# GpSimd subtracts weights instead of scaling probabilities in a two-layer attention and MLP trunk, with projection blocks in another order

## The chip, the cores and the metric

The kernel runs on one core of one Trainium2 chip. The metric is the device time of one execution in microseconds (us). The kernel before takes 627.66 us, the median of three runs (627.09 to 627.96).

## What is computed

The reference is a trunk of two layers on 256 tokens of width 1024, all in float32. A layer normalizes its input, projects it to 2848 columns, runs two kinds of attention on the parts, projects the result back, and follows with an MLP whose activation is a squared ReLU:

```python
for l in range(DEPTH):                                   # DEPTH = 2
    h = _rms_norm(x, g_pre_mix[l])
    parts = jnp.split(h @ w_in[l], split_at, axis=-1)
    nq, kc, vc, ksel, vsel, kwin, vwin, gates, fq, fk, fv, ff = parts
    ...
    mix = jnp.concatenate([o_nsa, o_fox], axis=-1) @ w_out[l]
    x = x + _rms_norm(mix, g_post_mix[l])
    h = _rms_norm(x, g_pre_mlp[l])
    y = jnp.square(jax.nn.relu(h @ w_up[l])) @ w_down[l]
    x = x + _rms_norm(y, g_post_mlp[l])
```

The first kind of attention, "nsa", has eight heads of 64 columns in two groups. Each head adds three branches, each with a gate: attention to compressed keys and values (16 blocks, made by a small network with a GELU), to selected keys and to a window; with 256 tokens the last two see all earlier tokens, with different keys and values. The second kind, "fox", has eight heads with a decay that comes from running sums of forget gates. Queries and keys of nsa are rotated by position (RoPE).

## The kernel before, in words

**Products of float32 by three passes.** TensorE multiplies numbers in a shorter format (fp32r). A weight tile `wraw`, loaded by DMA, is therefore split: ScalarE copies it to `whi` in the short format, VectorE subtracts `wraw - whi` into `wlo` (`Weights.get`, L625; the subtraction is L648). Activations are split alike (`split`, L807). A product is the sum of three: high by high, high by low, low by high.

**The projection in blocks.** The first 2048 of the projection's columns come in 16 blocks of 128 (`block`, L1254): each is 8 matmuls of 512 columns with `whi` (which do both halves of the activation at once) and 8 of 256 with `wlo`, into one of two `acc` buffers of PSUM. The block is evacuated by a ScalarE copy and a VectorE add (`both_halves`, L970) to its home (`block_home`, L1192); only then is its `acc` buffer free for the block after next. The homes in order are `kT` (blocks 0, 1: selected and window keys), `cT` (2, 3: what the compressed keys and values are made of), `qT` (4 to 7: queries, two heads each), then `fqT` and `fkT` (8 to 15). In layer 0 the first four blocks are computed together while data arrives (`first_chunks`); in layer 1 the first two (`by_token`).

**Rotation** (`turned`, L976) of a pair of blocks takes a VectorE product `m`, a shuffle of it, a GpSimd product `y`, a VectorE sum, and a split into `kx` (keys) or `qS` (queries). `rCS` holds the cosines and sines times the norm of each token, and is made once in a layer.

**Attention** runs over 24 entries (`flat`): 16 of nsa, for four pairs of heads, two heads and two branches, then eight of fox. For each, `scores` (L1365) makes the scores of a pair on TensorE (the `kx,qS` or `cum` and `fkT,fqT` matmuls), subtracts the maximum on VectorE and exponentiates on ScalarE; `scale` (L1387) takes reciprocals and scales the probabilities `pr` in two pieces, 128x128 and 128x256; `probs_T` (L1403) transposes them on TensorE (`s<-cst,pr`); `values` multiplies by the values (`o<-prT`, `o<-prX`). The scaling is on GpSimd for fox and for the window branch (L1392, L1400), on ScalarE for the other. Between the steps `fill(n)` gives TensorE parts of the stream of blocks, of a last projection chunk (`c5`) and of the output projection; `fill_to(b)` gives it all up to block b. The compression steps (`side`, L1501) come at entries given by `SIDE`. The weights `cmp_w1` of the compression's network ride behind the blocks listed in `SEQ`.

**The order of all this is planned.** The code only records operations. `Recorder.order` then simulates the five engines with a price for every operation (`_cost`, L578), tries 140 orders with random shifts, and emits the best; each engine runs its instructions strictly in that order. So a change of a price or of the recorded sequence moves instructions on every engine. Prices in it know nothing of one engine that holds another off.

All instructions are recorded by one helper, so that almost every row of the profile has the line L535; tiles tell them apart.

Of the kernel before, what the change touches and what calls it, by code (L numbers as in the profile page):

```python
# [38 lines left out]
SEQ = range(7, 15), range(4, 12)  # L39
SIDE = (2, 7), (1, 5)  # L40
PV1 = 12
# [17 lines left out]
TM = FM + 288, FM + 512  # L59
TURNED = [i ^ 8 if i < 16 else i for i in range(32)]  # L60
# [517 lines left out]
def _cost(op, views):  # L578
    out = op.args[0] if op.args else op.kw["out"]
    n = int(np.prod(out.shape[1:]))  # L580
    if op.engine == "sync":
        v = views[0][1]
        return v.shape[0] * int(np.prod(v.shape[1:])) * 4 / 320.0
    if op.engine == "tensor":
        if op.name == "stretch":
            if op.args[2][0][0] == "transpose":
                return 108.0 * len(op.args[2])

            tiles = [_shape(x[1][1]) for x in op.args[2]]
            return sum((x[1][0].ix.size / (2.4 if x[1][1].dtype == F32R else 0.6) + 20) / (P // min(t))  # L590
                       for x, t in zip(op.args[2], tiles)) + RETILE * sum(a != b for a, b in zip(tiles, tiles[1:]))
        if op.name == "transpose":
            return 83.0 if op.args[1].dtype == F32R else 108.0
        if op.args[1].dtype == F32R:
            return 13.6 + n / 2.4
        return max(220.0, 3 + n / 0.6)
    if op.engine == "gpsimd":
        return 160 + n * (2.2 if op.name.startswith("tensor_tensor") or op.name == "tensor_mul" else 1.0)
    if op.engine == "vector":
        if op.name == "reciprocal":  # L600
            return 60 + 6.5 * n
        if op.name == "tensor_reduce":
            n = int(np.prod(op.args[1].shape[1:]))
        fast = op.name in ("tensor_copy", "tensor_scalar", "memset") and not any(v.buf.psum for _, v in views)
        aps = sum(isinstance(v, View) for v in op.args[2:4]) if op.name == "tensor_scalar" else int(
            op.name == "scalar_tensor_tensor" and isinstance(op.args[2], View))
        return 68 + 64 * aps + n * (0.52 if fast else 1.04) + 10 * (op.name == "tensor_tensor_reduce")
    src = op.args[1]
    aps = sum(isinstance(op.kw.get(k), View) for k in ("bias", "scale", "accum_out"))
    return n / 1.2 + (55 if src.buf.psum else 92) + 93 * aps  # L610


class Weights:
# [11 lines left out]
    def get(self, i):  # L625
# [14 lines left out]
        for j in range(shape[0]) if i < 2 * len(FIRSTS) else [slice(None)]:  # L640
# [7 lines left out]
            nc.vector.tensor_sub(lo[:, j], raw[:, j], hi[:, j].bitcast(F32))  # L648
# [16 lines left out]
def trunk(nc, A, consts_in, out, sbp, pp):  # L665
# [260 lines left out]
    for l in range(DEPTH):  # L926
# [47 lines left out]
        two = lambda x: x[:, None, :].to_broadcast([P, 2, S])  # L974

        def turned(src, hi, lo):  # L976

            m = tokt("m").rearrange("p (b n) -> p b n", b=2)
            y = tokt("y").rearrange("p (b n) -> p b n", b=2)
            nc.vector.tensor_mul(m, src, two(T["rS"]))  # L980
            nc.vector.stream_shuffle(m, m, TURNED)
            nc.gpsimd.tensor_mul(y, src, two(T["rC"]))
# [209 lines left out]
        def block_home(b):  # L1192

            name = ("kT", "cT", "qT", "qT", "fqT", "fqT", "fkT", "fkT")[b // 2]
            if name not in T:
                if b < 4:
                    T[name] = tokt(name).rearrange("p (b n) -> p b n", b=2)
                else:
                    T[name] = qT_tile(name)
# [4 lines left out]
            return T[name][:, b % 2 if b < 4 else b % 4, :]  # L1204

        def block_done(b):

            if b >= 8 and b % 2:
                d = T["fqT" if b < 12 else "fkT"][:, b % 4 - 1:b % 4 + 1, :]
                nc.vector.tensor_mul(d, T["u"], two(T["r"]))  # L1210
            if b in (5, 7):
                if b == 5:
                    T["qS"] = tile([P, 2, 4, S], F32R, name="qS", tag="gain")
                turned(T["qT"][:, b - 5:b - 3, :], *[T["qS"][:, j, b - 5:b - 3, :] for j in range(2)])
# [271 lines left out]
        b2k = rows[:, 36:37]  # L1486
        fill(4)
        turned(T["kT"], *kx)
        if not first:
            fill_to(3)  # L1490
        fill(4)
        gather_blocks(0)
        fill(4)
        gather_blocks(1)
        fill_to(5)
        fill(2)
# [6 lines left out]
                cv + 2: lambda: (compressed_T(), hidden_gelu("v")), cv + 3: compressed_v, 12: lambda: fill_to(NB - 1),  # L1503
                13: forget_sums, 16: lambda: fill_to("c5")}
# [5 lines left out]
        for i in range(len(flat) + 4):  # L1510
# [16 lines left out]
            fill(1)  # L1527
# [167 lines left out]
def layouts(a):  # L1695
# [6 lines left out]
    w = np.concatenate([ks, kw, kc, vc, by_head(q, 2), fox[:, :, :1024], vs, vw, by_head(g, 2), ff, fox[:, :, 1024:]],  # L1702
# [38 lines left out]
```

## Time and profile before

| what | value |
|---|---|
| median of three runs | 627.66 us |
| the profiled execution's own time | 628.2 us |
| its span, first to last instruction | 626.4 us |
| granted TensorE clock | 0.997 |
| TensorE's weight loads busy | 504.6 us, 81% |
| GpSimd busy | 78.6 us, 94 instructions |
| loaded from HBM | 114.30 MB |
| chain that ended last | PE 82%, DVE 7%, ACT 5%, issue 2%, POOL 2%, DMA 1% |

In the rows PE is TensorE's matmuls, PEld its weight loads, DVE VectorE, ACT ScalarE, POOL GpSimd. A row of a group names its output and inputs, their shapes and the count, then the busy us and the mean ns of one, then the engine's idle us just before them and what ended most of it. A row of the timeline begins with its start and its length in us; idle time ahead of it stands in brackets. Busy time of TensorE overlaps from matmul to matmul, and its ends are modelled.

### The profile page before, as it was taken

To read this page: it belongs to the slowest core of one execution; us is meant where nothing else is said; L and a number is where in the kernel's file an instruction comes from. 1 tells how busy PE (TensorE), PEld (TensorE's weight loads), DVE (VectorE), ACT (ScalarE), POOL (GpSimd) and SP (SyncE) were. 2 spreads that over 40 slices of the span, in tenths; PEclk is the share of its full clock that TensorE was granted. 3 is DMA by queue.
4 is the path that set the end of the run, shared out by engine and by line. 5 is a ranking of instruction groups with operands and counts; after the bars stand their busy time and mean duration, and the time that the engine had idled before them with its cause. 6 is when DMAs were issued, how large, how long until landed. Compare 5 with 4: busy or idle time off the path is not lost.

```text
span 626.4 us, 9901 instructions
## 1 busy us (share of the span) xinstructions
PE 608.8 (97%) x3488; PEld 504.6 (81%) x3488; DVE 457.9 (73%) x967; ACT 390.7 (62%) x802; POOL 78.6 (13%) x94
## 2 busy tenths in 40 slices
PE   9989999999999999999999999999999999999995
PEld 8867776678888888888888778867888888888884
DVE  6899985579976566566599998674997666566544
ACT  6768987467665455455466697874776555555422
POOL 0225124500000000000003432362000000000000
PEclk9999999999999999999999999999999999999998
DMA  8967774317756556555327657342486566555101
GB/s 287 402 239 257 296 225 135 102 35 265 261 190 204 188 181 201 193 182 187 133 83 253 236 171 275 102 169 68 131 290 211 176 196 202 180 191 203 37 0 68
DMA packets 36354, 115.99 MB, mean 185 GB/s; under 512 B 4432, under 2 KB 6224, under 8 KB 36304
## 3 DMA queue, kind: packets, MB, share of 16 engines
q1 hardware_dynamic: 36304, 115.36, 54.0%
q8 instruction: 27, 0.44, 0.3%
q14 instruction: 23, 0.19, 0.1%
HBM read 114.30 MB, written 1.05 MB: 184 GB/s over the span
## 4 chain that ended last, share of the span: by engine, by line
PE 82%; DVE 7%; ACT 5%; issue 2%; POOL 2%; DMA 1%; POOLq 0%; DVEq 0%; ACTq 0%
PE s L535 33%; PE acc L535 24%; PE x L535 18%; PE o L535 7%; POOL pr L535 2%; DVE wlo L535 2%; ACT whi L535 1%; ACT pr L535 1%; DVE m L535 1%; DMA wraw<-in_w_fm_dram 1%; DVE pr L535 1%; ACT rl L535 1%; ACT kstk L535 0%; DMA wraw<-in_w_dram 0%; POOLq L1737 0%
## 5 line engine op out<-in xcount | busy, mean ns | idle before, releaser
L535 DVE TENSOR_TENSOR wlo<-wraw,whi 128x1024 fp32r<-128x1024 f32 (+2 forms) x200 | 231.7, 1164 | 96.9 <-ACT whi L535 96.3
L535 ACT ACTIVATE whi<-wraw 128x1024 fp32r<-128x1024 f32 (+3 forms) x200 | 199.8, 1006 | 128.0 <-PE acc L535 61.4
L535 PE MATMUL s<-xT,whi 128*128 128x512 f32 x448 | 111.9, 392 | 0.0
L535 PEld LDWEIGHTS s<-xT,whi 128*128 128x128 f32 x448 | 81.4, 189 | 15.1
L535 PE MATMUL acc<-whi,aT 128*128 128x512 f32 x256 | 88.5, 390 | 0.0
L535 PE MATMUL x<-whi,aT 128*128 128x512 f32 x256 | 88.4, 390 | 0.0
L535 PE MATMUL acc<-xT,whi 128*128 128x512 f32 (+1 forms) x258 | 66.4, 385 | 2.7 <-DVE qT L535 2.0
L535 PEld LDWEIGHTS s<-xT,wlo 128*128 128x128 f32 x448 | 61.1, 190 | 4.4
L535 PE MATMUL s<-xT,wlo 128*128 128x256 f32 x448 | 62.5, 282 | 0.0
L535 ACT ACTIVATE pr<-pr,st 128x256 f32<-128x256 f32 (+1 forms) x128 | 55.3, 448 | 5.7 <-DVE st L535 5.4
L535 PEld LDWEIGHTS acc<-whi,aT 128*128 128x128 f32 x256 | 48.1, 188 | 10.0
L535 PEld LDWEIGHTS x<-whi,aT 128*128 128x128 f32 x256 | 48.1, 188 | 9.7
L535 PEld LDWEIGHTS acc<-xT,whi 128*128 128x128 f32 x258 | 43.6, 189 | 11.8 <-DVE qT L535 2.2
L535 PE MATMUL x<-wlo,aT 128*128 128x512 f32 x128 | 50.0, 390 | 0.0
L535 PE MATMUL acc<-wlo,aT 128*128 128x512 f32 x128 | 49.8, 389 | 0.0
L535 PE MATMUL acc<-xT,wlo 128*128 128x256 f32 x240 | 36.7, 284 | 0.0
L535 PEld LDWEIGHTS acc<-xT,wlo 128*128 128x128 f32 x240 | 33.3, 190 | 2.2 <-issue 0.4
L535 POOL TENSOR_TENSOR y<-kT,rCS 128x512 f32<-128x512 f32 x2 | 5.0, 2483 | 239.9 <-DVE rCS L535 239.9
L535 POOL TENSOR_SCALAR pr<-pr,st,gate 128x256 f32<-128x256 f32 (+1 forms) x32 | 25.7, 814 | 62.0 <-DVE st L535 56.0
L535 POOL TENSOR_SCALAR pr<-pr,st 128x128 f32<-128x128 f32 (+1 forms) x32 | 30.3, 964 | 22.3 <-DVE st L535 18.8
L535 PE MATMUL s<-cst,pr 128*128 128x128 f32 x144 | 24.3, 281 | 5.5 <-POOL pr L535 4.9
L535 ACT ACTIVATE rl<-h 128x512 f32<-128x512 f32 x28 | 17.5, 624 | 18.0 <-DVE h L535 18.0
(226 smaller groups left out, 921.9 us busy)
## 6 DMA issues: line engine op xcount, KB each, us to landing
wraw<-in_w_up_dram SPq DMA_DIRECT2D x64, 512.0 KB, 3.9
wraw<-in_w_down_dram SPq DMA_DIRECT2D x64, 512.0 KB, 3.5
wraw<-in_w_fm_dram SPq DMA_DIRECT2D x28, 512.0 KB, 6.3
wraw<-in_w_out_dram SPq DMA_DIRECT2D x16, 512.0 KB, 7.3
wraw<-in_w_dram SPq DMA_DIRECT2D x9, 512.0 KB, 4.0
w<-in_cmp_w_k_dram SPq DMA_DIRECT2D x8, 512.0 KB, 5.3
w<-in_cmp_w_v_dram SPq DMA_DIRECT2D x8, 512.0 KB, 6.4
wraw<-in_w_dram SPq DMA_DIRECT2D x6, 256.0 KB, 4.1
```

The lines of the kernel that those rows point to most:

```text
L535: getattr(getattr(self.nc, op.engine), name)(*[real(v) for v in args], **{k: real(v) for k, v in kw.items()})
```

## The change

It has six parts.

- `scale`: the scalings that GpSimd did, 64 instructions, are VectorE's. `turned`: the product `y`, six instructions, is VectorE's too.
- `Weights.get`: of blocks 7, 9, 11, 13 and 15 of each layer GpSimd does the subtraction `wraw - whi`, ten instructions of 128x1024.
- `HOMES`: the projection's columns are reordered so that block 3 is the first pair of queries and block 4 the compressed values; `fill_to((3, 5, 7, 7)[pair])` and a rotation of queries in pieces of one, one and two blocks (`q_turned`) follow from that.
- The compression's weights ride behind blocks 4 to 11 in layer 0 too, and its steps start at entries 4 and 9 in both layers.
- fox's scores call for their two blocks themselves (`fill_to(12 + (pair | 1))`), `c5` is called for at entry 18, the first nsa product by values comes at entry 14, and two parts of the stream are given at a step instead of one.
- `_cost`: GpSimd's instructions have other prices.

```diff
-SEQ = range(7, 15), range(4, 12)
-SIDE = (2, 7), (1, 5)
-PV1 = 12
+SEQ = range(4, 12), range(4, 12)
+SIDE = (4, 9), (4, 9)
+PV1 = 14
...
+HOMES = [("kT", 0), ("kT", 1), ("cT", 0), ("qT", 0), ("cT", 1), ("qT", 1), ("qT", 2), ("qT", 3)]
+HOMES += [(name, i) for name in ("fqT", "fkT") for i in range(4)]
...
-        return 160 + n * (2.2 if op.name.startswith("tensor_tensor") or op.name == "tensor_mul" else 1.0)
+        return {"tensor_mul": 700 + 2.5 * n, "tensor_sub": 700 + 3.2 * n, "tensor_copy": 600}.get(op.name, 550 + 2.2 * n)
...
-            nc.vector.tensor_sub(lo[:, j], raw[:, j], hi[:, j].bitcast(F32))
+            (nc.gpsimd if kind == "shared" else nc.vector).tensor_sub(lo[:, j], raw[:, j], hi[:, j].bitcast(F32))
...
-                add_unit((l, "in", c, q), [8, P], A["w_fm"][l, q])
+                add_unit((l, "in", c, q), [8, P], A["w_fm"][l, q], "shared" if q > 5 and q % 2 else "split")
...
-            nc.gpsimd.tensor_mul(y, src, two(T["rC"]))
+            nc.vector.tensor_mul(y, src, two(T["rC"], n))
...
-                turned(T["qT"][:, b - 5:b - 3, :], *[T["qS"][:, j, b - 5:b - 3, :] for j in range(2)])
+                q_turned(*((1, 2) if b == 5 else (2, 4)))
...
+                    fill_to(12 + (pair | 1))
...
-                    fill_to(4 + (pair | 1))
+                    fill_to((3, 5, 7, 7)[pair])
...
-                    nc.gpsimd.tensor_scalar(p[:, a:b], p[:, a:b], st[:, 2 + t:3 + t], None, op0=OP.mult)
+                    nc.vector.tensor_scalar(p[:, a:b], p[:, a:b], st[:, 2 + t:3 + t], None, op0=OP.mult)
...
-                    nc.gpsimd.tensor_scalar(p[:, a:b], p[:, a:b], st[:, 2 + t:3 + t], gate[t][:, c:c + 1],
+                    nc.vector.tensor_scalar(p[:, a:b], p[:, a:b], st[:, 2 + t:3 + t], gate[t][:, c:c + 1],
...
-        fill_to(5)
-        fill(2)
+        fill(8)
...
-                cv + 2: lambda: (compressed_T(), hidden_gelu("v")), cv + 3: compressed_v, 12: lambda: fill_to(NB - 1),
-                13: forget_sums, 16: lambda: fill_to("c5")}
+                cv + 2: lambda: (compressed_T(), hidden_gelu("v")), cv + 3: compressed_v,
+                13: forget_sums, 18: lambda: fill_to("c5")}
...
-            fill(1)
+            fill(2)
```

What this makes of the emitted order is shown at three places. First GpSimd, in layer 0 from its first instruction on tensors: rotations `y`, copies that gather `kstk` and `kstv` for the compression, and the scalings of `pr`. Before:

```order
L535 TENSOR_TENSOR y<-kT,rCS 128x512
L535 COPY kstk<-rows 128x32
L535 COPY kstv<-rows 128x32
L535 TENSOR_TENSOR y<-qT,rCS 128x512
L535 COPY kstk<-cT 64x8x15 x4
L535 COPY kstk<-rows 128x32
L535 TENSOR_SCALAR pr<-pr,st,gate 128x256
L535 TENSOR_SCALAR pr<-pr,st,gate 128x128
L535 COPY kstv<-cT 64x8x15 x4
```

After, from the same place (the first `wlo` is that of block 7, the next three of blocks 9, 11 and 13, then 15 and layer 1's 7):

```order
L537 TENSOR_TENSOR wlo<-wraw,whi 128x1024
L537 COPY kstk<-rows 128x32
L537 COPY kstv<-rows 128x32
L537 COPY kstk<-cT 64x8x15 x4
L537 COPY kstv<-cT 64x8x15 x4
L537 COPY kstk<-rows 128x32
L537 TENSOR_TENSOR wlo<-wraw,whi 128x1024 x3
L537 COPY kstv<-rows 128x32
L537 TENSOR_TENSOR wlo<-wraw,whi 128x1024 x2
```

The `y` and the scalings are gone from GpSimd, and a subtraction stands ahead of its first copy. Second, VectorE in layer 0 from `rCS` on, where keys and the first queries are rotated and blocks are evacuated (`qT<-acc`). Before:

```order
L535 TENSOR_TENSOR rCS<-cst,rT 128x512
L535 TENSOR_TENSOR wlo<-wraw,whi 128x1024
L535 TENSOR_TENSOR m<-kT,rCS 128x512
L535 TENSOR_TENSOR qT<-acc,qT 128x256
L535 TENSOR_TENSOR wlo<-wraw,whi 128x1024
L535 TENSOR_TENSOR m<-qT,rCS 128x512
L535 STREAM_SHUFFLE m<-m 128x512 x2
L535 TENSOR_TENSOR y<-y,m 128x512 x2
L535 TENSOR_TENSOR qT<-acc,qT 128x256
L535 TENSOR_TENSOR kx<-y,kx 128x512
L535 TENSOR_TENSOR qS<-y,qS 128x512
```

After, from the same `rCS` to the first evacuation behind it, that of block 5:

```order
L537 TENSOR_TENSOR rCS<-cst,rT 128x512
L537 TENSOR_TENSOR wlo<-wraw,whi 128x1024
L537 TENSOR_TENSOR m<-kT,rCS 128x512
L537 TENSOR_TENSOR y<-kT,rCS 128x512
L537 STREAM_SHUFFLE m<-m 128x512
L537 TENSOR_TENSOR m<-qT,rCS 128x256
L537 TENSOR_TENSOR y<-y,m 128x512
L537 STREAM_SHUFFLE m<-m 128x256
L537 TENSOR_TENSOR y<-qT,rCS 128x256
L537 TENSOR_TENSOR qT<-acc,qT 128x256
```

Before, that evacuation stands behind one `m`, after behind two `m`, two `y` and the shuffles; the rotation of the queries has half the width. Third, TensorE where the first pair's scores (`kx,qS`) stand in layer 0. Before, in block 8:

```order
L535 MATMUL acc<-xT,whi 128x512 x6
L535 MATMUL s<-kx,qS 128x256 x6
L535 MATMUL x<-kx,qS 128x512 x6
L535 MATMUL acc<-xT,whi 128x512 x2
L535 MATMUL acc<-xT,wlo 128x256 x8
L535 MATMUL o<-w_325,kstk 32x256 x4
```

After, in block 7 (the first row is its `whi` part):

```order
L537 MATMUL acc<-xT,whi 128x512 x8
L537 MATMUL acc<-xT,wlo 128x256 x3
L537 MATMUL s<-kx,qS 128x256 x6
L537 MATMUL x<-kx,qS 128x512 x6
L537 MATMUL acc<-xT,wlo 128x256 x5
L537 MATMUL acc<-xT,whi 128x512 x4
L537 MATMUL o<-w_345,kstk 32x256 x4
```

The scores stand five `wlo` and six `whi` matmuls earlier, and the first matmuls of the compression's network (`w,kstk`) come in the middle of block 8 instead of behind it.

More of the change, by code (lines that the diff above doesn't have):

```diff
@@ L972, in both_halves @@
             nc.vector.tensor_add(dst, ps[:, :S], dst)
-        two = lambda x: x[:, None, :].to_broadcast([P, 2, S])
+        two = lambda x, n=2: x[:, None, :].to_broadcast([P, n, S])
         def turned(src, hi, lo):
-            m = tokt("m").rearrange("p (b n) -> p b n", b=2)
-            y = tokt("y").rearrange("p (b n) -> p b n", b=2)
-            nc.vector.tensor_mul(m, src, two(T["rS"]))
+            n = src.shape[1]
+            m, y = (tokt(x)[:, :n * S].rearrange("p (b n) -> p b n", b=n) for x in "my")
+            nc.vector.tensor_mul(m, src, two(T["rS"], n))
             nc.vector.stream_shuffle(m, m, TURNED)
-            nc.gpsimd.tensor_mul(y, src, two(T["rC"]))
+            nc.vector.tensor_mul(y, src, two(T["rC"], n))
             nc.vector.tensor_add(y, y, m)
@@ L1192, in block_home @@
         def block_home(b):
-            name = ("kT", "cT", "qT", "qT", "fqT", "fqT", "fkT", "fkT")[b // 2]
+            name, i = HOMES[b]
             if name not in T:
[L1196 to L1199, printed above, removed]
+                T[name] = tokt(name).rearrange("p (b n) -> p b n", b=2) if name in ("kT", "cT") else qT_tile(name)
             if b >= 8:
@@ L1203, in block_home, with q_turned @@
                 return T["u"][:, b % 2, :]
-            return T[name][:, b % 2 if b < 4 else b % 4, :]
+            return T[name][:, i, :]
         def block_done(b):
             if b >= 8 and b % 2:
-                d = T["fqT" if b < 12 else "fkT"][:, b % 4 - 1:b % 4 + 1, :]
-                nc.vector.tensor_mul(d, T["u"], two(T["r"]))
+                name, i = HOMES[b]
+                nc.vector.tensor_mul(T[name][:, i - 1:i + 1, :], T["u"], two(T["r"]))
             if b in (5, 7):
-                if b == 5:
-                    T["qS"] = tile([P, 2, 4, S], F32R, name="qS", tag="gain")
-                turned(T["qT"][:, b - 5:b - 3, :], *[T["qS"][:, j, b - 5:b - 3, :] for j in range(2)])
+                q_turned(*((1, 2) if b == 5 else (2, 4)))
+        def q_turned(a, b):
+            if a == 0:
+                T["qS"] = tile([P, 2, 4, S], F32R, name="qS", tag="gain")
+            turned(T["qT"][:, a:b, :], *[T["qS"][:, j, a:b, :] for j in range(2)])
         def first_chunks():
@@ L1305, in part @@
                 done.add(name)
+            done.update(range(4 if first else 2))
             for b in range(4 if first else 2, NB):
@@ L1486, in trunk @@
         b2k = rows[:, 36:37]
+        if not first:
+            fill_to(2)
         fill(4)
@@ L1490, in trunk @@
             fill_to(3)
+        q_turned(0, 1)
         fill(4)
         gather_blocks(0)
-        fill(4)
+        fill_to(4)
         gather_blocks(1)
-        fill_to(5)
-        fill(2)
+        fill(8)
         flat = [("nsa", pair, par, br) for pair in range(4) for par in range(2) for br in (1, 2)]
@@ L1701, in layouts @@
     by_head = lambda x, axis: np.take(x.reshape(*x.shape[:axis], 8, -1, *x.shape[axis + 1:]), order, axis=axis).reshape(x.shape)
-    w = np.concatenate([ks, kw, kc, vc, by_head(q, 2), fox[:, :, :1024], vs, vw, by_head(g, 2), ff, fox[:, :, 1024:]],
+    q = by_head(q, 2)
+    w = np.concatenate([ks, kw, kc, q[:, :, :128], vc, q[:, :, 128:], fox[:, :, :1024], vs, vw, by_head(g, 2), ff, fox[:, :, 1024:]],
                        axis=2)
```

## The prediction

> **What bounds the kernel now.** I read the page's busy table first, then the windows by stage, then TensorE's own waits, then the timeline at the longest of them.
>
> ```profile
> PE 608.8 (97%) x3488; PEld 504.6 (81%) x3488; DVE 457.9 (73%) x967; ACT 390.7 (62%) x802; POOL 78.6 (13%) x94
> ```
>
> TensorE is busy for 608.8 of 626.4 us, so a change that leaves its matmuls alone can win at most its 17.6 idle us. The windows (columns: stage, length, then busy us of PE, PEld, DVE, ACT, POOL, the granted clock, DMA share and GB/s) say where those are. 25 to 135 us is the attention of layer 0, 335 to 435 us that of layer 1, and what follows each is MLP.
>
> ```profile
> 25.00:50.00 25.00, 21.02 (x147) 16.80 (x146) 24.19 (x59) 16.77 (x41) 10.37 (x12) 1.00 0.79 294
> 50.00:100.00 50.00, 50.00 (x350) 39.67 (x350) 45.19 (x147) 44.63 (x119) 13.99 (x20) 1.00 0.73 249
> 100.00:135.00 35.00, 32.95 (x213) 23.59 (x211) 19.52 (x58) 21.63 (x61) 13.90 (x16) 1.00 0.25 82
> 135.00:335.00 200.00, 199.90 (x1027) 170.69 (x1027) 146.50 (x217) 114.76 (x178) 0.00 (x0) 1.00 0.56 187
> 335.00:360.00 25.00, 24.14 (x165) 19.49 (x164) 23.53 (x72) 15.38 (x45) 12.41 (x13) 1.00 0.65 231
> 360.00:400.00 40.00, 40.00 (x319) 33.15 (x320) 34.13 (x123) 34.27 (x102) 10.67 (x13) 1.00 0.58 201
> 400.00:435.00 35.00, 32.73 (x217) 23.80 (x214) 19.82 (x54) 23.05 (x60) 17.08 (x18) 1.00 0.36 121
> ```
>
> TensorE idles in four of them: 4.0 us in 25 to 50, 2.1 in 100 to 135, 0.9 in 335 to 360, 2.3 in 400 to 435. In the first and third VectorE is full (24.2 and 23.5 of 25 us); in the second and fourth nobody is, so there a chain of latencies is late. The MLP has nothing to win. TensorE's waits, with total us, times and the longest:
>
> ```profile
> PE s L535 <- POOL pr L535: 4.9, 6, 1.2
> PE acc L535 <- DVE qT L535: 2.0, 1, 2.0
> PE acc L535 <- ACT whi L535: 0.8, 1, 0.8
> PE s L535 <- ACT pr L535: 0.5, 1, 0.5
> PE s L535 <- DVE hs L535: 0.4, 1, 0.4
> ```
>
> These five rows, 8.6 us, are all that this change can reach. The timeline of TensorE places the first three:
>
> ```profile
> 31.29 2.00 PE L535 MATMUL acc<-xT,whi 128*128 128x512 f32 x8
> 33.13 1.11 PE L535 MATMUL acc<-xT,wlo 128*128 128x256 f32 x8
> 36.22 1.65 PE L535 MATMUL acc<-xT,whi 128*128 128x512 f32 x6 [1.98 <-DVE qT L535]
> 49.76 0.55 PE L535 MATMUL s<-cst,pr 128*128 128x128 f32 x3 [1.25 <-POOL pr L535]
> ```
>
> 1.25 of the 4.9 us behind GpSimd's `pr` stand in the crowded start of layer 0; the other five waits, 3.65 us, are the ends of the two attentions. Why the wait for `qT` is there shows on VectorE and GpSimd in the same microseconds:
>
> ```profile
> 26.66 0.68 DVE L535 TENSOR_TENSOR rCS<-cst,rT 128x512 f32<-128x512 f32 x1
> 27.26 1.23 DVE L535 TENSOR_TENSOR wlo<-wraw,whi 128x1024 fp32r<-128x1024 f32 x1
> 28.41 1.79 DVE L535 TENSOR_TENSOR m<-kT,rCS 128x512 f32<-128x512 f32 x1
> 27.42 2.22 POOL L535 TENSOR_TENSOR y<-kT,rCS 128x512 f32<-128x512 f32 x1 [27.00 <-DVE rCS L535]
> L535 DVE TENSOR_TENSOR m<-qT,rCS x4: 626/1224/1781, 31.6 to 351.4; 128x512 f32<-128x512 f32 x4
> 52.32 1.29 POOL L535 TENSOR_TENSOR y<-qT,rCS 128x512 f32<-128x512 f32 x1
> 52.51 1.15 DVE L535 TENSOR_SCALAR gz<-gz 128x64 f32<-128x64 f32 x1
> 55.69 0.19 DVE L535 TENSOR_SCALAR gz<-gz 128x64 f32<-128x64 f32 x1
> ```
>
> VectorE's multiply `m` of 512 columns takes between 626 and 1781 ns. The long ones ran beside GpSimd's `y`: `y` was issued at 27.42, sat through VectorE's `wlo`, won the moment that ended (28.49), ran 1.15 us to 29.64, and `m` came after. A one-input `gz` of 64 columns, 0.19 us alone, took 1.15 beside a `y`. So one instruction holds the other off for its whole length, and a GpSimd two-input instruction costs VectorE up to 1781 - 626 = 1155 ns per 512 columns. The two held `m` (2.2 us) are the 1.98 us for which TensorE waited: the `qT` evacuation that frees its accumulator is queued behind them.
>
> **The change part by part.** (1) *Scaling of probabilities moves from GpSimd to VectorE*, 64 instructions, and six `y` with it.
>
> ```profile
> L535 POOL TENSOR_SCALAR pr<-pr,st 128x256 f32<-128x256 f32 x16 | 17.6, 1106 | 9.5 <-DVE st L535 6.0 <-PE acc L535 3.5
> L535 POOL TENSOR_SCALAR pr<-pr,st 128x128 f32<-128x128 f32 x16 | 13.1, 822 | 12.8 <-DVE st L535 12.8
> L535 DVE COPY hs<-o 128x256 f32<-128x256 f32 x4 | 1.7, 415 | 0.0
> L535 DVE TENSOR_SCALAR vS<-o,rsqrt 128x128 f32<-128x128 f32 x2 | 0.7, 344 | 0.0
> L535 DVE TENSOR_TENSOR wlo<-wraw,whi 128x1024 fp32r<-128x1024 f32 x180 | 220.0, 1226 | 95.2 <-ACT whi L535 94.8
> L535 DVE TENSOR_TENSOR y<-y,m 128x512 f32<-128x512 f32 x6 | 4.0, 679 | 0.0
> L535 DVE STREAM_SHUFFLE m<-m 128x512 f32<-128x512 f32 x6 | 4.3, 741 | 0.0
> ```
>
> On GpSimd a head's two scalings follow each other, 1106 + 822 = 1.93 us. VectorE has no SBUF scaling of these sizes in the trace. From below the 64-column `gz`, 0.19, bounds each of the two; from above the 256-column copy and the 128-column scaling out of PSUM, 0.42 + 0.34 = 0.76 us a head; I take 0.55, nearer the upper rows. So the chain of each scaled head is about 1.4 us shorter, while VectorE gets 32 x 0.55 = 17.6 us more work (12 to 24), and 6 x 0.68 = 4.1 for `y`. At the two ends VectorE is busy 19.5 and 19.8 of 35 us, which covers its half. The 3.65 us of waits there go; what is late next is the last pair's scaling behind `xo` and the gains product in VectorE's queue, which I price at 0.5 (0 to 3.65).
>
> (2) *Ten `wlo` subtractions move to GpSimd.* VectorE is rid of 10 x 1.23 = 12.3 us. A GpSimd subtraction of 1024 columns is not in the trace; by the `y` rows it holds VectorE for 2 x 1.15 = 2.3 us, an estimate, at worst, and for nothing where VectorE is just then at work on PSUM. Queued behind a held VectorE instruction is all of its queue, the accumulator evacuations among it, and for those TensorE waits. [...]
>
> (3) *The new order at the start of layer 0*, the place that matters most.
>
> ```profile
> 26.18 2.00 ACT L535 ACTIVATE whi<-wraw 128x1024 fp32r<-128x1024 f32 x2
> 334.27 0.68 DVE L535 TENSOR_TENSOR rCS<-cst,rT 128x512 f32<-128x512 f32 x1
> 342.91 2.00 PE L535 MATMUL acc<-xT,whi 128*128 128x512 f32 x8
> ```
>
> VectorE's chain up to the evacuation of block 5 (`qT<-acc` after the products for `kT` and the first query block) now holds their `y` too. A VectorE row starts some 0.08 us before the one ahead of it ends (26.66 + 0.68 against 27.26), so the steps are `rCS` 0.60, `wlo` 1.15, `m` and `y` 0.60 each, shuffle 0.65, a 256-column `m` 0.33 (the 415 ns of the copy less 0.08), the sum into `y` 0.60, half a shuffle 0.40, a 256-column `y` 0.33: 5.26 us. From 26.66 that is 31.9, and with the evacuation's 0.41 it is 32.3. TensorE reaches block 7 at 31.29 and needs that accumulator for it. So it waits 1.1 us even if nobody holds VectorE. GpSimd's first subtraction is block 7's; its `whi` is the second of ScalarE's two from 26.18 and done at 28.2, while VectorE is in `wlo`, just the spot in which `y` won before. I charge the full 2.3: 3.4 us of wait at block 7 (1.1 to 3.4) where 1.98 stood at block 8. The scores are then ready with block 7's third `wlo` matmul, as the order has them: nothing more.
>
> (4) *The first pair's probabilities in layer 0.* The 1.25 us behind `pr` go. VectorE's scaling is ready about 0.5 us before TensorE wants it, if the second subtraction (block 9) doesn't fall into those microseconds; if it does, 1.8 us are lost. I take 0.7. Of the 0.8 us behind `whi` I keep 0.2, since TensorE reaches block 9 later.
>
> (5) *Layer 1's start.* From `rCS` at 334.27 seventeen instructions, 7.1 us by the same steps, stand ahead of the evacuation that block 6 needs: it ends at 341.7, and TensorE comes at 342.91. With 1.2 us to spare the 0.9 us of waits there go; a full hold leaves 1.1. I take 0.8 for all.
>
> (6) *The middle stretches* (50 to 100, 360 to 400) had no wait, with VectorE idle for 4.8 and 5.9 us. Seven subtractions fall in these or near their edges. What they take from VectorE beyond what they relieve, 2.3 - 1.23 = 1.1 us each, is covered by that idle time; without that cover it is 7.7 us. I take 0.6.
>
> (7) *The rest*: compression steps at other turns, loads in another sequence (the eight `cmp_w` blocks ride earlier) and GpSimd's new planning prices touch only order. DMA is 79% busy in 25 to 50 us and nothing of TensorE waits for a landing there, so I cost them at nothing; if that cover fails, a late block costs about the 0.8 us that one `whi` cost.
>
> Sum: waits after = 3.4 + 0.7 + 0.2 + 0.8 + 0.6 + 0.5 = 6.2 us for 8.6, a gain of 2.4. The profiled execution took 628.2 us (1.8 outside its span), so 625.8 by its own time; it lies 0.54 over the median of 627.66, which gives **625.3 us**.
>
> **The rivals.** *Holds decide (slower).* Nine subtractions besides block 7's cost TensorE what they net cost VectorE: 9 x 1.1 = 9.9 us in place of the 2.1 that I gave them. Waits become 14.0, the time 628.2 + 5.4 - 0.54 = 633.1; at half that price 628.1. It is slower by the bound below from 0.64 us per subtraction on. For it: VectorE is full in the two starts (24.2 and 23.5 of 25 us) and is given 22 us more while relieved of 12. Against: TensorE had not one wait in 50 to 100 us with VectorE at 90%. Chance 0.21.
>
> *The waits change names (no change).* At the ends TensorE waits as long for VectorE's `pr`, because in-order VectorE puts `xo`, gains and `wlo` ahead of it, or layer 0's start costs 2 us more than I gave it. Waits stay near 8.6: 627.7. For it: the ends are chains, where the next link is always close. Against: 1.4 us less per head in them. Chance 0.21.
>
> *GpSimd does the waiting (faster still).* If VectorE wins the lock whenever both want it, the holds vanish from its side, and only 1.1 + 0.2 + 0.5 remain: 8.6 - 1.8 = 6.8 us gained, 620.9.
>
> ```profile
> 404.10 5.59 POOL L535 TENSOR_SCALAR pr<-pr,st 128x256 f32<-128x256 f32 x4 [3.40 <-DVE st L535]
> 405.58 3.72 DVE L535 TENSOR_TENSOR wlo<-wraw,whi 128x1024 fp32r<-128x1024 f32 x3 [0.78 <-ACT whi L535]
> ```
>
> For it: here four scalings took 5.59 us beside three undisturbed `wlo`. Against: two of the four `m` beside a `y` lost. Chance 0.12.
>
> **How the numbers follow.** The forecast, between 623 and 627, has 0.46. A measurement of this kernel tells about 0.2% from no change, 1.25 us. Of the forecast 0.43 lies below 626.4 and 0.03 above; with the faster rival that makes faster 0.55, no change 0.24, slower 0.21. The range 620.3 to 630.0 takes in the forecast, no change, the faster rival, and the slower one to about half its price; it leaves out some 0.15.
>
> **What would show it.** Right: TensorE's waits behind `POOL pr` are gone, `PE s` waits at the two ends are under 0.5 us in all, block 7's first matmul near 31.3 us waits about 3.4 us for VectorE's `qT`, and GpSimd's `wlo` rows take between 2.3 and 4.5 us, with long VectorE rows beside them. The forecast is wrong if the busy us of TensorE move by more than 1, if waits in 50 to 100 us exceed 2 us, or if the ends still wait for `pr`; block 7 waiting under 1.5 us would say that VectorE wins the lock.

## The result, and the profile after

The changed kernel takes 634.26 us, the median of 12 executions (630.36 to 636.66), beside 627.9 for the kernel before on the same chip. The ratio of the means is 1.0089 (95% interval 1.0063 to 1.0114): slower, where faster by 0.4% was forecast, and outside the range that was given. The 12 executions fall into two groups by the granted TensorE clock: four took 630.4 to 630.5 us at a mean clock of 0.996 to 0.999, eight took 633.8 to 636.7 at 0.987 to 0.993. Both are slower than before. The profiled one belongs to the second: 634.56 us, with a span of 632.6.

The busy row of the changed kernel's page:

```profile
PE 612.8 (97%) x3488; PEld 508.4 (80%) x3488; DVE 479.7 (76%) x1039; ACT 390.6 (62%) x804; POOL 37.9 (6%) x34
```

The span is 6.2 us longer: TensorE idles for 19.8 us in place of 17.6, and is busy for 4.0 us longer with the same 3488 matmuls. The second part was in no sum of mine. The windows by stage (columns as before: length, busy us of PE, PEld, DVE, ACT, POOL, clock, DMA share, GB/s):

```profile
25.00:50.00 25.00, 21.19 (x144) 16.35 (x142) 24.09 (x71) 16.98 (x45) 11.62 (x13) 0.93 0.79 288
50.00:100.00 50.00, 47.35 (x341) 36.76 (x342) 48.09 (x169) 40.19 (x117) 7.58 (x4) 1.00 0.66 223
100.00:135.00 35.00, 35.00 (x215) 27.25 (x212) 23.01 (x60) 21.37 (x52) 0.00 (x0) 1.00 0.35 120
335.00:360.00 25.00, 21.49 (x142) 16.55 (x140) 24.53 (x67) 16.46 (x45) 13.72 (x11) 1.00 0.51 176
360.00:400.00 40.00, 38.77 (x270) 31.23 (x271) 38.16 (x127) 31.37 (x90) 4.80 (x2) 0.96 0.64 221
400.00:435.00 35.00, 35.00 (x268) 27.61 (x267) 28.77 (x96) 26.01 (x71) 0.00 (x0) 1.00 0.38 129
```

The two ends (100 to 135, 400 to 435) now have no idle time at all: that part came as forecast. Everything ahead of them got worse, and two windows show a clock under 1. TensorE's waits on its timeline:

```profile
35.49 3.58 PE L537 MATMUL acc<-xT,whi 128*128 128x512 f32 x8 [3.07 <-DVE qT L537]
47.82 0.72 PE L537 MATMUL acc<-xT,whi 128*128 128x512 f32 x2 [0.74 <-DVE qT L537]
54.79 0.67 PE L537 MATMUL s<-cst,pr 128*128 128x128 f32 x3 [0.75 <-DVE pr L537]
65.13 0.55 PE L537 MATMUL s<-cst,pr 128*128 128x128 f32 x3 [1.25 <-ACT pr L537]
...
352.31 2.11 PE L537 MATMUL acc<-xT,whi 128*128 128x512 f32 x8 [0.44 <-DVE qT L537]
358.72 0.50 PE L537 MATMUL acc<-xT,whi 128*128 128x512 f32 x1 [1.49 <-DVE qT L537]
359.96 0.46 PE L537 MATMUL s<-cst,pr 128*128 128x128 f32 x1 [0.73 <-ACT pr L537]
```

Block 7 waits 3.07 us, as forecast (3.4), but its eight matmuls then take 3.58 us where eight such took 2.00 before. VectorE's rows show what it was doing ahead of these waits:

```profile
29.38 2.88 DVE L537 TENSOR_TENSOR m<-kT,rCS 128x512 f32<-128x512 f32 x1
...
61.48 0.41 DVE L537 TENSOR_TENSOR rl<-acc,rl 128x256 f32<-128x256 f32 x1
61.81 0.15 DVE L537 RECIPROCAL st<-st 128x2 f32<-128x2 f32 x1
61.88 2.23 DVE L537 TENSOR_TENSOR fqT<-rl,rT 128x512 f32<-128x512 f32 x1
...
70.01 2.15 DVE L537 TENSOR_SCALAR pr<-pr,st,gate 128x256 f32<-128x256 f32 x1
...
348.34 3.58 DVE L537 TENSOR_TENSOR wlo<-wraw,whi 128x1024 fp32r<-128x1024 f32 x1
...
352.97 2.62 DVE L537 TENSOR_TENSOR y<-qT,rCS 128x256 f32<-128x256 f32 x1
...
383.77 1.88 DVE L537 TENSOR_TENSOR st<-st,gate 128x2 f32<-128x2 f32 x1
```

And GpSimd's subtractions in the same places:

```profile
29.23 2.49 POOL L537 TENSOR_TENSOR wlo<-wraw,whi 128x1024 fp32r<-128x1024 f32 x1 [28.79 <-ACT whi L537]
61.17 2.39 POOL L537 TENSOR_TENSOR wlo<-wraw,whi 128x1024 fp32r<-128x1024 f32 x1 [6.61 <-ACT whi L537]
69.45 2.56 POOL L537 TENSOR_TENSOR wlo<-wraw,whi 128x1024 fp32r<-128x1024 f32 x1 [1.34 <-ACT whi L537]
336.05 3.76 POOL L537 TENSOR_TENSOR wlo<-wraw,whi 128x1024 fp32r<-128x1024 f32 x1 [264.04 <-ACT whi L537]
348.45 2.39 POOL L537 TENSOR_TENSOR wlo<-wraw,whi 128x1024 fp32r<-128x1024 f32 x1
352.69 2.61 POOL L537 TENSOR_TENSOR wlo<-wraw,whi 128x1024 fp32r<-128x1024 f32 x1
383.25 2.39 POOL L537 TENSOR_TENSOR wlo<-wraw,whi 128x1024 fp32r<-128x1024 f32 x1 [5.87 <-ACT whi L537]
```

Each of VectorE's long rows here ends 0.01 to 1.08 us after GpSimd's, which is 0.1 to 0.3 us less than its own undisturbed length: 61.17 + 2.39 = 63.56, and `fqT`, 0.68 us by itself, ends at 64.11; 383.25 + 2.39 = 385.64, and the product into `st`, 0.15 us by itself, ends at 385.65. The trace has such a row beside every one of the ten subtractions: eight with two SBUF inputs, and the scalings at 52.24 and 70.01 us. That product, of 128x2, is the smallest of them, and took 1.88 us. Rows with one operand in PSUM (`rl<-acc,rl`, 0.41 us, where the 16 of its kind have a mean of 0.42) and a `RECIPROCAL` (0.15 us, where 48 have a mean of 0.16) pass meanwhile. The two scalings, which stood still as well, have one SBUF tensor as input.

The granted clock, in finer windows behind the two longest waits:

```profile
34.00:36.00 2.00, 0.51 (x2) 0.41 (x3) 2.00 (x8) 0.83 (x2) 0.00 (x0) 0.94 1.02 418
36.00:38.00 2.00, 2.00 (x6) 1.53 (x5) 2.00 (x7) 1.95 (x7) 1.41 (x2) 0.50 0.85 342
38.00:40.00 2.00, 2.00 (x14) 1.65 (x14) 1.97 (x7) 1.94 (x5) 1.92 (x4) 0.71 0.06 25
...
360.00:362.00 2.00, 1.68 (x7) 1.39 (x8) 2.00 (x5) 1.94 (x7) 0.00 (x0) 0.50 0.90 305
362.00:364.00 2.00, 2.00 (x12) 1.24 (x12) 2.00 (x9) 1.18 (x3) 0.00 (x0) 0.65 1.07 389
```

Twice the clock is 0.5 for about 3.4 us. What is lost is (0.06 + 0.50 + 0.29) x 2 = 1.7 us the first time and (0.50 + 0.35) x 2 = 1.7 the second. TensorE itself waited for 0.32 us of the second, so these are about 3.2 of the 4.0 us by which it is busy for longer.

### The profile page after: what moved, and what is told of

It reads as the page before. It is cut to its first block, busy times and chain, and to the rows that moved or that the text cites. A ratio compares the mean times of both kernels' runs of the same rounds, so it can differ in the third digit from the quotient of the medians.

```text
span 632.6 us, 9864 instructions
## 1 busy us (share of the span) xinstructions
PE 612.8 (97%) x3488; PEld 508.4 (80%) x3488; DVE 479.7 (76%) x1039; ACT 390.6 (62%) x804; POOL 37.9 (6%) x34
## 4 chain that ended last, share of the span: by engine, by line
PE 81%; DVE 13%; ACT 2%; issue 1%; DMA 1%; SPq 0%; DVEq 0%; ACTq 0%
PE s L537 33%; PE acc L537 22%; PE x L537 19%; PE o L537 7%; DVE wlo L537 3%; DVE pr L537 2%; DVE m L537 2%; ACT pr L537 1%; DVE y L537 1%; DMA wraw<-in_w_dram 1%; DVE st L537 1%; DVE fqT L537 1%; ACT whi L537 0%; DVE x L537 0%; SPq L537 0%
## 5 line engine op out<-in xcount | busy, mean ns | idle before, releaser
L537 DVE TENSOR_TENSOR wlo<-wraw,whi 128x1024 fp32r<-128x1024 f32 (+3 forms) x190 | 223.5, 1182 | 93.0 <-ACT whi L537 92.3
L537 PE MATMUL acc<-xT,whi 128*128 128x512 f32 (+1 forms) x258 | 70.3, 398 | 7.3 <-DVE qT L537 5.7
L537 PEld LDWEIGHTS acc<-xT,whi 128*128 128x128 f32 x258 | 45.2, 194 | 18.0 <-DVE qT L537 6.8
L537 POOL TENSOR_TENSOR wlo<-wraw,whi 128x1024 fp32r<-128x1024 f32 x10 | 25.8, 2577 | 331.4 <-ACT whi L537 331.3
L537 PE MATMUL acc<-xT,wlo 128*128 128x256 f32 x240 | 38.1, 287 | 0.0
L537 ACT ACTIVATE rl<-x 128x512 f32<-128x512 f32 x24 | 14.7, 614 | 24.2 <-PE x L537 17.8
L537 PEld LDWEIGHTS acc<-wlo,aT 128*128 128x128 f32 x128 | 24.0, 188 | 4.9
L537 PEld LDWEIGHTS x<-wlo,aT 128*128 128x128 f32 x128 | 24.1, 188 | 4.4
```

The lines of the kernel that those rows point to most:

```text
L537: getattr(getattr(self.nc, op.engine), name)(*[real(v) for v in args], **{k: real(v) for k, v in kw.items()})
```

## The experiments

Each was compared with the kernel before on one chip, with medians of 628.3 to 628.8 for it there, so a difference between two rows is good to about half a microsecond (an estimate by that spread). The ratios are of means. The table gives, beside the medians, TensorE's busy and idle us in each profiled execution, which need not be the median one.

| kernel | median us | ratio to before (95%) | busy | idle |
|---|---|---|---|---|
| before | 627.9 | | 608.8 | 17.6 |
| changed | 634.26 | 1.0089 (1.0063 to 1.0114) | 612.8 | 19.8 |
| 1 changed, subtractions on VectorE | 624.31 | 0.9944 (0.9925 to 0.9963) | 607.8 | 14.4 |
| 2 changed, two waits filled | 630.65 | 1.0033 (1.0021 to 1.0045) | 613.8 | 15.1 |
| 3 before, 14 waits put in | 679.27 | 1.0809 (1.0795 to 1.0823) | 629.6 | 48.3 |
| 4 before, subtractions on GpSimd | 639.64 | 1.0176 (1.0157 to 1.0195) | 615.4 | 23.7 |
| 5 before, scalings and `y` on VectorE | 625.35 | 0.9946 (0.9934 to 0.9959) | 610.3 | 13.6 |
| 6 changed, four subtractions back | 626.48 | 0.9973 (0.9965 to 0.9982) | 610.9 | 15.0 |
| 7 changed, six subtractions back | 628.36 | 1.0004 (0.9995 to 1.0013) | 610.1 | 16.3 |
| 8 as 1, one evacuation earlier | 624.41 | 0.9948 (0.9935 to 0.9962) | 608.2 | 14.1 |
| 9 as 1, GpSimd subtracts too | 650.26 | 1.0344 (1.0325 to 1.0363) | 619.6 | 27.9 |
| 10 changed, planned without GpSimd's | 619.32 | 0.9854 (0.9837 to 0.9871) | 606.5 | 11.0 |
| 11 before, 5 planned anew | 620.50 | 0.9871 (0.9854 to 0.9888) | 608.1 | 10.9 |
| 12 as 10, subtractions on GpSimd | 630.24 | 1.0033 (1.002 to 1.0046) | 609.3 | 19.0 |

Where an engine is "swapped", the plan is left as it is and only the engine of an instruction is exchanged when it is emitted, so that all other engines keep their order row for row. That tells the price of an instruction from the price of another plan.

### 1. The subtractions swapped back

```diff
-                    getattr(getattr(self.nc, op.engine), name)(
+                    getattr(getattr(self.nc, "vector" if name == "tensor_sub" else op.engine), name)(
```

> The changed kernel with one thing undone: the ten subtractions run on VectorE, each at the place in VectorE's queue at which GpSimd's was planned; the order of TensorE, ScalarE and the loads is that of the changed kernel to the letter. Theory A (the holds): each GpSimd subtraction takes up to 2.2 us from VectorE where VectorE's own takes 1.15, and the waits of both starts and of layer 0's middle come from that. Block 7's wait then falls from 3.07 to about 2.0 us, layer 1's waits for qT (1.49) and pr (0.73) mostly go, TensorE's waits fall from 11.7 to 6 to 8 us, no stretch shows a granted clock under 0.98, and the median is 627 to 629. Theory B (the order): VectorE's queue is too full of work there, whoever subtracts; giving it ten subtractions of 1.15 us more leaves the waits at 11 us or more and the median at 633 or above.

It took 624.31 us, 10 us less than the changed kernel: theory A, and by more than it gave. VectorE's busy time, on the page:

```profile
PE 607.8 (98%) x3488; PEld 506.0 (81%) x3488; DVE 471.6 (76%) x1049; ACT 390.0 (63%) x804; POOL 13.2 (2%) x24
```

VectorE did ten more instructions, 12.2 us of work by the 1.22 of a `wlo`, and was busy for 8.1 us less: the ten holds had taken 20.3 us, 2.0 each. Block 7 waits 2.03 us now, a little less than the forecast's 1.1 and one `wlo`.

### 2. The long waits filled

The numbers in `FILLS` are the place in the plan, the kind of tile written, and the count.

```diff
+FILLS = {315: ("s", 12), 2765: ("s", 6)}
...
+                if i in FILLS:
+                    ...
+                    for _ in range(n):
+                        self.nc.tensor.matmul(b.real, x[:, :P], x, start=True, stop=True)
```

> The changed kernel, with matmuls that nobody reads put into TensorE's queue at two of its waits: 12 of 512 columns (2.6 us) ahead of block 7 in layer 0, 6 (1.3 us) behind the 32 compression products at 357 us in layer 1. They end before the awaited tile is there, so the waits stay as long, only filled. Theory C (the clock): the 4.0 us by which TensorE is busy for longer are a granted clock of 0.5 for about 3.4 us after each of these waits, and it is granted for lack of work. Filled, the eight matmuls of block 7 take 2.0 us again in place of 3.58, the clock stays at 1.0 in 36 to 40 us and in 360 to 364, and the median falls by 3 to 4 us, to 630 to 631. Rival D (contention): the matmuls after the waits are slow because GpSimd, VectorE and the loads press on SBUF there; then they stay slow and the median stays at 634, or rises by what the filling delays.

TensorE's timeline and its clock:

```profile
31.84 2.91 PE L547 MATMUL s<-xT 128*128 128x512 f32 x12
35.09 2.11 PE L539 MATMUL acc<-xT,whi 128*128 128x512 f32 x8 [0.34 <-DVE qT L539]
```

```profile
36.00:38.00 2.00, 2.00 (x17) 1.66 (x17) 2.00 (x8) 1.93 (x6) 1.76 (x3) 1.00 0.30 121
38.00:40.00 2.00, 2.00 (x16) 1.49 (x15) 1.95 (x5) 1.96 (x5) 1.96 (x3) 1.00 0.04 8
360.00:362.00 2.00, 2.00 (x17) 1.26 (x15) 2.00 (x10) 1.70 (x6) 0.00 (x0) 1.00 1.03 420
```

Eighteen matmuls more, and 3.6 us less: 630.65, with all six executions between 630.4 and 631.0. Block 7's eight take 2.11 us with VectorE as full as before, and at the second place the clock stays whole at a DMA share of 1.03, so theory D is out: with the waits filled the clock is 1.00 in 36 to 38 and in 360 to 362 us, where the changed kernel had 0.50. By their granted clocks such falls are also the difference between the changed kernel's two groups of executions, though none of the faster group has a trace.

### 3. Waits of known length, elsewhere

```diff
+STALLS = dict(zip((1279, 1435, ...), 2 * [1, 2, 3, 4, 5, 6, 7]))
...
+                    self.nc.vector.tensor_copy(d, last)
+                    for _ in range(STALLS[i] - 1):
+                        self.nc.vector.tensor_copy(d, d)
+                    self.nc.tensor.matmul(b.real, d[:, :P], d, start=True, stop=True)
```

> The kernel before with 14 waits put into its two MLPs, seven in each: TensorE must take up a matmul (one more, of 512 columns) that needs a chain of 1, 2, 3, 4, 5, 6 or 7 copies of VectorE, begun when TensorE has finished the block ahead. The waits should be some 0.5 us plus 0.35 to 0.65 us per copy, 1 to 4.5 us. What is asked is the granted clock behind each. [...] Theory D (no clock, contention): the blocks behind the waits take as long as ever. The time is that of the kernel before plus the waits (30 to 40 us) plus 1.7 us per fall.

The waits came out at 1.12 to 3.64 us. Some of them on TensorE's timeline:

```profile
203.47 0.47 PE L540 MATMUL s<-d 128*128 128x512 f32 x1 [1.80 <-DVE d L539]
229.80 0.47 PE L540 MATMUL s<-d 128*128 128x512 f32 x1 [2.26 <-DVE d L539]
282.28 0.47 PE L540 MATMUL s<-d 128*128 128x512 f32 x1 [3.18 <-DVE d L539]
```

The clock behind these three:

```profile
205.00:207.00 2.00, 2.00 (x7) 1.61 (x7) 0.00 (x0) 0.32 (x1) 0.00 (x0) 0.50 0.72 246
231.00:233.00 2.00, 2.00 (x14) 1.80 (x13) 0.13 (x1) 0.85 (x1) 0.00 (x0) 1.00 0.59 186
284.00:286.00 2.00, 2.00 (x8) 1.61 (x7) 0.00 (x0) 0.24 (x1) 0.00 (x0) 0.50 0.83 258
```

Over all 14, read in windows of 1 us: behind the waits of 1.12 to 1.34 us the clock stayed at 1.0 (four of four), behind 1.80 it fell (two of two), behind 2.26 it stayed (two of two), behind 2.72, 3.18 and 3.64 it fell (six of six). Each fall was to 0.5 for about 3.4 us. TensorE was busy for 20.8 us longer than before, of which the 14 added matmuls are 6.6; 14.2 over eight falls is 1.8 us each. So theory D is out here too: the eight `s<-xT,whi` behind the wait of 2.72 us at 255 us took 3.18 us, those behind the wait of 1.12 at 158 us 2.00. The length of a wait alone doesn't decide, since 1.80 us did it and 2.26 did not; what does was not shown. It is the same elsewhere: behind a wait of 2.02 us at block 7 in layer 0 the clock was 0.50 in 36 to 38 us (kernel 6), behind one of 2.03 it was 1.00 throughout 25 to 50 us (kernel 1).

### 4 and 5. One part of the change alone, in the order of before

In the first diff `shared` marks the ten subtractions; the lines that set it are left out.

```diff
-                    getattr(getattr(self.nc, op.engine), name)(
+                    getattr(getattr(self.nc, "gpsimd" if getattr(op, "shared", False) else op.engine), name)(
```

```diff
-                    getattr(getattr(self.nc, op.engine), name)(
+                    getattr(getattr(self.nc, "vector" if name in ("tensor_scalar", "tensor_mul") else op.engine), name)(
```

> The kernel before, with the ten subtractions alone moved to GpSimd, each at the place where VectorE did it; TensorE, ScalarE and loads in the order of before. GpSimd still scales the probabilities. My prediction's price (a hold is covered outside block 7) gives at most 1 us more, 628 to 629. Theory A (each hold costs TensorE what it costs VectorE, 1.1 us) gives up to 11 us more, 633 to 639, with long VectorE rows beside GpSimd's wlo and waits of TensorE behind them; scalings queued on GpSimd behind a 2.6-us subtraction come on top of it in both.

> The kernel before, with the scalings of probabilities and the products y alone moved from GpSimd to VectorE, at their places; TensorE, ScalarE and loads in the order of before. If the prediction's first part is right, the waits behind GpSimd's pr (4.9 us) and the two held m behind block 8 (2.0) mostly go, VectorE is busy for about 28 us more (0.73 us a head, 0.68 a y), and the median is 622 to 625. The rival: VectorE, 90% busy in 50 to 100 us, becomes late there; new waits behind it eat the gain and the median is 627 or above.

The subtractions alone cost 1.76%, 11 us: theory A's figure (639.64, just over its 633 to 639), but not by its mechanism alone. In the profiled execution, whose span is 12.7 us longer, TensorE idles for 6.1 us more and is busy for 6.6 more, and 5.1 of the latter went to a clock of 0.5 in 37.5 to 41.5 and 362 to 369 us. Some of the idle time is scalings that queue behind the subtractions on GpSimd (TensorE's waits behind `POOL pr` rose from 4.9 to 6.4 us). The scalings and `y` alone gained 0.54%, 3.4 us: close to what the forecast said of the ends (3.65 less 0.5), and 0.35 us short of the 622 to 625 expected here.

### 6 and 7. Which of the ten

The diff is that of kernel 6, without the lines that pass the mark on; kernel 7 has `q > 10`, and what is marked "back" is emitted on VectorE.

```diff
-"shared" if q > 5 and q % 2 else "split"
+("shared back" if q < 10 else "shared") if q > 5 and q % 2 else "split"
```

> The changed kernel with four of its ten GpSimd subtractions, those of blocks 7 and 9 in both layers, run on VectorE at their planned places, and the six of blocks 11, 13 and 15 left on GpSimd; every order as in the changed kernel. All ten on VectorE gave 624.3, all ten on GpSimd 634.3, 630.4 where the granted clock did not fall. Theory P (each costs about the same): six of ten cost 3.7 us, 628.0, and up to 1.7 more in runs whose clock falls. Theory Q (my sum: only those in the crowded starts cost, the later ones are covered by VectorE's idle time): 624.3 to 625.5, with no new wait over 0.5 us in 50 to 100 and 360 to 400 us.

> The complement: blocks 7 and 9 of both layers on GpSimd, blocks 11, 13 and 15 on VectorE, orders as in the changed kernel. Theory P: four of ten cost 2.5 us, 626.8, and the clock still falls behind block 7's wait in most runs, which makes 628 to 629. Theory Q: nearly all of the cost is here, 630 with the clock up and 632 to 634 where it falls.

Six late ones cost 2.2 us over kernel 1, four early ones 4.1: 0.4 and 1.0 each. In the fastest execution of each (625.98 and 627.36 beside 623.95), where the clock had fallen least, it is 2.0 and 3.4. So neither theory holds whole: the early ones are dearer, but the late ones, five of them in stretches that had no wait before, are not free. Together they make 6.2 us, and 624.3 + 6.2 is 630.5, where the changed kernel's first group has 630.4 to 630.5. That fit is partly luck: the median of kernel 7 has falls of the clock in it (1.7 us in its profiled execution, behind a wait of 3.07 at block 7), and the fastest executions add up to 5.4.

### 8. One evacuation ahead

The swap of kernel 1 stands here too.

```diff
-            for op in self.order():
+            for op in (lambda ops: ops.insert(296, ops.pop(321)) or ops)(self.order()):
```

> The changed kernel with all subtractions on VectorE (624.3), and one instruction of VectorE's queue moved: the evacuation of block 5, for which TensorE still waits 2.03 us ahead of block 7 in layer 0, stands ahead of block 7's subtraction and of the seven steps for kT and the first query block. If that wait is mere order, it goes; the first scores then wait up to 1 us for qS, whose chain is as long as before, and the median is 623.0 to 623.6, with fewer runs whose clock falls. If the wait is full use of VectorE, the scores wait the whole 2 us and the median stays at 624.3.

```profile
31.35 2.00 PE L537 MATMUL acc<-xT,whi 128*128 128x512 f32 x8
33.19 0.51 PE L537 MATMUL acc<-xT,wlo 128*128 128x256 f32 x3
34.52 0.38 PE L537 MATMUL s<-kx,qS 64*128 64x256 f32 x2 [0.82 <-ACT qS L537]
35.06 0.39 PE L537 MATMUL s<-kx,qS 64*128 64x256 f32 x2 [0.15 <-DVE qS L537]
35.85 0.38 PE L537 MATMUL s<-kx,qS 64*128 64x256 f32 x2 [0.41 <-DVE kx L537]
```

Block 7 doesn't wait any more; the scores wait 1.38 us in its stead, and block 9 still 1.27. The time stays, 624.41. In this order VectorE's queue is full there, and a single row moved only moves the wait.

### 9. GpSimd subtracts what nobody needs

The swap of kernel 1 stands here too, and the line that names the pool is left out.

```diff
+                    if name == "tensor_sub" and op.engine == "gpsimd":
+                        j = self.pool.tile([P, 8, P], F32R, name="j", tag="j", bufs=1)
+                        self.nc.gpsimd.tensor_sub(j, *[real(v) for v in args[1:]])
```

> The changed kernel with all ten subtractions done on VectorE (624.3), and GpSimd doing the same ten as well, at its old places, into a tile that nobody reads. Theory A (the lock): what costs time is that VectorE stands still while GpSimd subtracts, whoever needs the result; each GpSimd subtraction then shows a VectorE row beside it that is some 2.2 us too long, and the median is 630 or above, more than the changed kernel's own if the clock falls as often, since VectorE has its ten besides. Theory E (lateness): GpSimd takes 2.6 us where VectorE takes 1.2, and its results come late; with nobody waiting for them the median stays at 624 to 625. Tiles of raw weights are held until GpSimd is done in both, as in the changed kernel.

650.26 us, 26 more than without them: theory A, and much more than it gave. Lateness can't be it, since nothing reads `j`. TensorE idles for 13.5 us longer than in kernel 1 and is busy for 11.8 longer, with waits of up to 4.3 us and a mean clock of 0.979; five stretches at a clock of 0.5 make up the 11.8. How much of it is the later release of raw weight tiles was not told apart.

### 10 and 11. The same work, planned anew

Kernel 10 is the changed kernel with `"split"` for every block; kernel 11 is the kernel before with `nc.vector` in place of `nc.gpsimd` for the scalings and `y`.

> The changed kernel with no block marked for GpSimd's subtraction, so that the planner knows it and orders all engines anew. If the order that was planned around GpSimd's prices has a cost of its own, it beats the 624.3 us of the same work in the old order, by up to 2 us (the waits of 2.0 and 1.2 us for qT in layer 0); if not, 623.5 to 625. Its random trials alone can move it by 1 us either way.

> The kernel before with the scalings of probabilities and the products y recorded for VectorE, and planned anew: the change without its subtractions and without its new order of blocks. In the old plan this gave 625.35. If the new order of blocks is worth something, this stays at 624.5 to 626, above the 624.3 of the changed kernel with its subtractions on VectorE; if the move of the scalings is all, it comes to 624.3 or below.

619.32 and 620.50: both beat both kernels, by more than I had expected. Kernel 1, the plan made around GpSimd's prices with the subtractions then swapped to VectorE, takes 5.0 us more than a plan made for VectorE (624.3 and 619.3, the same work on the same engines). The new order of blocks is worth about 1.2 us, as far as the planner's random trials let one say; the move of the scalings, planned for, 1.3%.

### 12. The swap in the best order

The emission of kernel 4, on kernel 10.

> The order of the fastest kernel here (the changed kernel planned with all subtractions on VectorE, 619.3 us), kept to the letter on TensorE, ScalarE and the loads, with the ten subtractions swapped to GpSimd at their places. It asks whether a GpSimd subtraction costs as much in a plan that had no room for it. Theory A (the lock costs about the same anywhere that VectorE is full): by the 6.1 us that the swap was worth in the changed kernel's order, clock left out, 625 to 626, and up to 629 where the granted clock falls; VectorE's busy time goes up although ten subtractions leave it. The rival (the lock was dear only because the changed kernel's plan had put the subtractions into the starts): under 622.

Busy rows of kernel 10, and of this one:

```profile
PE 606.5 (98%) x3488; PEld 505.9 (82%) x3488; DVE 471.2 (76%) x1049; ACT 390.6 (63%) x804; POOL 10.7 (2%) x24
```

```profile
PE 609.3 (97%) x3488; PEld 507.2 (81%) x3488; DVE 475.2 (76%) x1039; ACT 390.4 (62%) x804; POOL 38.2 (6%) x34
```

630.24, 10.9 us more: 1.09 for each subtraction, with the clock nearly whole (0.993 to 0.998). In the profiled executions TensorE idles for 8.0 us more, and a single fall of the clock (356.5 to 360.5 us) costs 1.7. Theory A at nearly twice its own figure of 6.1; in this plan, which had no room for it, a hold is dearer than in the changed kernel's (1.09 us beside 0.6). It also ends where the changed kernel's first group does, 630.4, so by these two orders planning around the subtractions gained nothing that shows. VectorE loses ten instructions, 12.2 us, and is busy for 4.0 longer.

## Why the prediction was wrong

**Right.** The ends: the waits for `pr` went, and VectorE's cover held (idle 0 in both, where I left 0.5). Moving the scalings and `y` gains 3.4 us in the old order (kernel 5). Block 7: 3.07 us of wait for my 3.4, and behind it the hold was 2.88 - 0.69 = 2.2 us for my 2.3. The first pair's `pr`: 0.75 for my 0.7, though in part by luck, since the subtraction that held it (52.17 us) was block 11's and not block 9's, and block 9's matmuls waited 0.74 elsewhere. GpSimd's rows took 2.4 to 3.8 us, and none of TensorE's waits names GpSimd's `pr`.

**Mis-sized, without weight.** VectorE scales a head in 0.39 + 0.34 us with a gate and 0.35 + 0.28 without, 0.68 on average for my 0.55.

**Wrong: step (6), the cover of the middle stretches, and step (5) with it.** I charged one subtraction in full and let VectorE's idle 4.8 and 5.9 us cover what the seven in and near the middle take net, 0.6 in all. All ten held VectorE, and the cover was partial: the six late ones cost 2.2 us by kernel 6. Layer 1's start waits 3.83 us (0.43 + 0.42 + 0.44 + 1.49 + 0.73 + 0.32) where I had 0.8: three subtractions run there, those at 348.45 and 352.69 held `wlo` and `y` one after the other, and I had let one fall there. Not all of it is holds: kernel 1 still waits 1.9 us in that start (0.28 + 0.24 + 1.39). In 50 to 100 us TensorE idles for 2.65 where my terms allowed 0.7 for the first pair and 0.6 for the middle of both layers. The cover was an average over 50 us, and a hold doesn't choose its time: at 61.17 us GpSimd started when ScalarE's `whi` was done, `fqT`, at 61.88, took 2.23 us for its 0.68, and the rows behind it in VectorE's queue started only then, at 64.03. Two of my signs for a wrong forecast came: over 2 us of waits in 50 to 100, and TensorE's busy time moved by more than 1.

**Wrong: a term that wasn't there.** I took TensorE's busy time as fixed. The waits at 35 and 358 us cost 1.7 us each beyond themselves by the clock (kernels 2 and 3). Even the 3.4 us that I forecast for block 7 belongs to the lengths that did this (2.72 to 3.64 us, six of six in kernel 3).

**The ledger.** My sum gave 625.8 us for the profiled execution, which took 634.56: 8.8 more. Of these, 3.0 are waits in layer 1's start (3.83 for 0.8), 2.1 those of the middles (1.9 and 0.81 for 0.6), 0.5 block 9, and 4.0 TensorE's longer busy time; block 7 and the ends came 0.3 and 0.5 below my terms.

**Not settled: step (7).** I put the new planning prices at nothing, as order only. Kernel 1 beside kernel 10 says 5.0 us for that order, kernel 12 beside the changed kernel less than 1 (629.6 to 629.9 at a clock of 0.998, beside 630.4).

**The rival that decided.** "Holds decide" gave 633.1 with 1.1 us for each subtraction, VectorE's net loss handed on to TensorE. Swapping them costs 1.0 each in the changed order with the clock's falls and 0.6 without; in the best order it is 1.1, of which 0.8 are waits of TensorE, and in the old one 1.1, of which 0.6 are. So its price for a wait was too high in the changed order, and that its 633.1 came so near 634.3 is partly luck: the clock, which it did not have, made up for it. What I held against it, that TensorE had no wait there with VectorE at 90%, was no evidence: it says nothing of a queue that stops for 2 us at a stroke.

**Where the changed kernel's 634.3 come from,** then: 619.3 for its work and block order planned without GpSimd's subtractions; 5.0 for an order planned around them at prices that know no hold; 6.1 for the holds; 3.9 for the clock (634.3 less the 630.4 of the executions with the highest clock). The last three are the subtractions' own, 15 us, and the rest of the change is a gain of 1.5%. How the 15 split depends on the path: by kernel 12, in the other order, the swap alone costs 10.9 (one fall of the clock in it), and planning around it less than 1.

## What to carry to other kernels

Before moving an elementwise instruction with SBUF inputs to GpSimd, charge its whole length there (2.4 us for a subtraction here) to VectorE's queue, at the moment when it starts, wherever the stage has VectorE near full and rows of the kinds that stood still here; idle time averaged over the stage covered only a part (the six late ones still cost 2.2 us). A wait of TensorE can have a second price behind it: 1.7 us here behind 3.07 us, and behind 1.49 and 0.73 close together, and filling two such places brought 3.6 us back. And swap the engine at a fixed order before judging a re-planned kernel, in more than one order: in the order planned around them the holds looked like 6 us and the plan like 5, in the other the swap alone cost 11.

## What the runs showed of the hardware

- VectorE stood still beside a GpSimd subtraction for up to its whole 2.4 us (`wlo` at 348.34 us: 3.58 for 1.22), down to a product of two columns (1.88 us for 0.15), and by form: beside eight of the ten a row with two SBUF inputs stood still, beside two a `tensor_scalar` on SBUF in float32 (2.15 us for 0.39); a row with an operand in PSUM (0.41 us, as by itself) and a reciprocal (0.15) went through.
- TensorE's clock fell to half for about 3.4 us behind some of its waits: of those put into the MLPs none of the four of 1.12 to 1.34 us, both of 1.80, neither of 2.26, and all six of 2.72 to 3.64; 18 unread matmuls in two waits of the changed kernel brought 3.6 us back.
